# Weight splits of the token-major products written 32 bytes past a multiple of 64

## The chip, the cores and the metric

The kernel runs on one core of a Trainium2 chip. The metric is the device time of one execution in microseconds (us); lower is better. Three runs of the kernel before gave 1770.18 to 1772.55 us, with a median of 1770.89.

## The reference

One layer of a hybrid block on 256 tokens of width 2048, all in float32. A normalised input is multiplied by a wide matrix; the pieces go through four branches (a gated linear recurrence, attention with forgetting, a state-space scan, an RWKV recurrence); each branch's output is projected, gated and summed; then an output projection, a feed-forward part with a short convolution, and a gated embedding follow. Cut to the products:

```python
xn = rmsnorm(h, mix_norm[i])
proj = jnp.einsum('bsd,dn->bsn', xn, w_in[i])        # 14092 columns: gates, a, b, c, d
...
gates = jax.nn.sigmoid(g_raw).reshape(Bsz, S, N_BRANCH, D)
merged = gates[:, :, 0] * jnp.einsum('bsc,cd->bsd', branches[0], w_branch[i, 0])
for j in range(1, N_BRANCH):
    merged = merged + gates[:, :, j] * jnp.einsum('bsc,cd->bsd', branches[j], w_branch[i, j])
h = h + jnp.einsum('bsd,de->bse', merged, w_out[i])
...
u = causal_dwconv(jnp.einsum('bsd,df->bsf', hn, w_up[i]), ffn_conv_w[i], ffn_conv_b[i])
h = h + jnp.einsum('bsf,fd->bsd', jax.nn.gelu(u_gate) * u_val, w_down[i])
pg = jax.nn.sigmoid(jnp.einsum('bsd,de->bse', rmsnorm(h, ple_norm[i]), w_ple_gate[i]))
h = h + pg * jnp.einsum('bsq,qd->bsd', p[i], w_ple[i])
```

## The kernel before

Weights come from DRAM in chunks of 128 partitions by 1024 float32 (tile `wr`, four buffers, queue of SyncE). Every chunk is split in two float32r parts by `split` (line 213): ScalarE casts it to `wh` (line 217), VectorE writes the remainder to `wl` (line 218), each with three buffers. Activations are split in the same way, so that a product of float32 numbers becomes three float32r products: high by high, high by low and low by high.

There are two kinds of product, and both end in `mm`, whose matmuls carry line 132. Every matmul has a stationary operand of 128 by 128, loaded by an instruction of its own, and a moving one.

- `gemm_fm` (line 261), feature-major: the weights are stationary and the activations move. A tile `x`, `f`, `e` or `d` holds the high part of the 256 tokens and, behind it, the low part, so that `product` (line 244) needs one matmul of 512 columns with `wh` and one of 256 columns with `wl`. From the second k-tile on the order is `wl` (256), `wh` (512), so short and long matmuls alternate; two 512s meet where one output tile or one unit ends and the next begins.
- `gemm_tm` (line 309), token-major: the activations are stationary and the weights move. For each of the two token tiles and each of two k-tiles in a chunk there are three matmuls of 512 columns: `wh`, `wh`, `wl`. A chunk has 12. It serves the projection `w_v`, the gates `w_g` (16 units) and the branch projections `w_branch` (16 units), which together lie between about 160 and 835 us.

In the profile's rows the operand that moves is named first: `pg<-x,wh` moves `x` over a stationary `wh` (feature-major), `pg<-wh,x` moves `wh` over a stationary `x` (token-major). `sb` are buffers of the branches; `pg` and `pb` are banks of PSUM.

Priorities of a scheduler set the order of instructions on each engine: the weights' loads and splits (`lane("g")`) first, then the branches' work (`lane("b")`), then the products (`lane("m")`); the branches' matmuls are laid into the products' stream by `on_pe` (line 130).

Where operands lie: in the program as built, `wr`, `wh` and `wl` start at multiples of 64 bytes in their partition. An 8-column tile (`pad0`, line 162, 32 bytes) stands ahead of the pools of activations, so `x`, `f`, `e`, `d`, `s` and `sb` start 32 bytes past a multiple of 64; slices of them are whole multiples of 64 bytes apart. `cbr` and `R` start at multiples of 64.

Of the kernel before, what the change touches and what calls it, by code (L numbers as in the profile page):

```python
# [8 lines left out]
F32R = mybir.dt.float32r  # L9
# [5 lines left out]
P = 128  # L15
# [70 lines left out]
def body(tc, T, out, dbg=None):  # L86
# [51 lines left out]
    def mm(o, l, r, start=True, stop=True):  # L138
        on_pe(PE.matmul, o, l, r, start=start, stop=stop)
# [11 lines left out]
    def lane(name):  # L151
        prio[cur[0]] = tc.cur_priority
        cur[0] = name
        tc.cur_priority = prio[name]
# [3 lines left out]
    wp = ctx.enter_context(tc.tile_pool(name="wp", bufs=2))  # L158
# [20 lines left out]
    def gbank():  # L179
        return psG.tile([P, 512], F32, name="pg", tag="pg")  # L180
# [27 lines left out]
    def chunk(src, kn, cols, eng=None):  # L208
        wr = wp.tile([P, kn, cols], F32, name="wr", tag="wr", bufs=4)
        (eng or dma_w).dma_start(wr, src)  # L210
        return wr

    def split(wr, kn, cols):

        wh = wp.tile([P, kn, cols], F32R, name="wh", tag="wh", bufs=3)
        wl = wp.tile([P, kn, cols], F32R, name="wl", tag="wl", bufs=3)
        A.copy(wh, wr)  # L217
        V.tensor_tensor(wl, wr, wh.bitcast(F32), op=ALU.subtract)  # L218
        return [(wh[:, i], wl[:, i]) for i in range(kn)]
# [21 lines left out]
    def halves(x):  # L241
        return (x[:, :S], x[:, S:]) if not isinstance(x, tuple) else x
# [18 lines left out]
    def gemm_fm(W, xs, evac, each=None):  # L261
# [12 lines left out]
        while k0 < nk:  # L274
            kn = min(step, nk - k0)
            lane("g")
            if each is not None:
                kn = 1 if k0 < 4 else 2
            if each is None:
                w = chunk(W[k0 // step].rearrange("p (k n) -> p k n", k=kn), kn, ncol)  # L280
            else:
                w = chunk(W[k0:k0 + kn].rearrange("k p n -> p k n"), kn, ncol)
                each(k0, kn)
            w = split(w, kn, ncol)
            lane("m")
            for m in range(nm):
                ms = slice(m * P, m * P + P)
                for k in range(kn):
                    if not isinstance(xs[k0 + k], tuple):
                        product(pts[m], xs, k0 + k, nk, ms, w[k], not (each and m == 0))  # L290
                        continue
                    xh, xl = xs[k0 + k]
                    wh, wl = w[k]
                    first, last = k0 + k == 0, k0 + k == nk - 1
                    pt = pts[m][:, :S]
                    mm(pt, wh[:, ms], xh, start=first, stop=False)
                    mm(pt, wh[:, ms], xl, start=False, stop=False)
                    mm(pt, wl[:, ms], xh, start=False, stop=last)
                if hook[0]:
                    hook[0]()  # L300
            k0 += kn
# [7 lines left out]
    def gemm_tm(W, xs, evac):  # L309

        nk = len(xs)
        pts = [gbank() for _ in range(2)]
        for k0 in range(0, nk, 2):
            lane("g")
            w = split(chunk(W[k0 // 2].rearrange("p (k n) -> p k n", k=2), 2, 512), 2, 512)
            lane("m")
            for t in range(2):
                tsl = slice(t * P, t * P + P)
                for k in range(2):
                    xh, xl = halves(xs[k0 + k])  # L320
                    wh, wl = w[k]
                    first, last = k0 + k == 0, k0 + k == nk - 1
                    mm(pts[t], xh[:, tsl], wh, start=first, stop=False)
                    mm(pts[t], xl[:, tsl], wh, start=False, stop=False)
                    mm(pts[t], xh[:, tsl], wl, start=False, stop=last)
                if hook[0]:
                    hook[0]()
        lane("g")
        for t in range(2):
            evac(t, pts[t])  # L330
        lane("b")
# [688 lines left out]
    def small_logits():  # L1020
        lane("g")
        wt = []
        for i in range(2):
            wt += split(chunk(T["w_small"][i].rearrange("p (k n) -> p k n", k=8), 8, 64), 8, 64)
        lane("m")
        pt = gbank()
        for k in range(KD):
            xh, xl = halves(xs[k])
            wh, wl = wt[k]
            mm(pt[:64, :S], wh, xh, start=k == 0, stop=False)  # L1030
            mm(pt[:64, :S], wh, xl, start=False, stop=False)
            mm(pt[:64, :S], wl, xh, start=False, stop=k == KD - 1)
        lane("b")
        bcol = pc("logit_bias", 0)[:64]
        y = bslot()
        tt(y[:64], pt[:64, :S], R[:64], ALU.mult)
        ts(y[:64], y[:64], bcol, cc("sgn")[:64], ALU.add, ALU.mult)
        o = bc_.tile([64, S], F32, name="spo")
        w = [bslot()[:64] for _ in range(5)]
        softplus(y[:64], o, w)  # L1040
        spf = bc_.tile([4, S], F32, name="spf")
        A.copy(spf, o[32:36])
        raw["sp_dt"] = o[0:8]
        raw["sp_f"] = spf
# [50 lines left out]
    def evac_v(t, pt):  # L1095
        s = dslot()
        act(s, pt, AF.Identity, scale=rcol[:, t:t + 1])
        raw["v"].append(s)
    gemm_tm(T["w_v"], xs, evac_v)
    launch("b", fox)  # L1100
    proj("du", 12, 7)
# [11 lines left out]
    def gate_unit(j, u, early):  # L1113
        def ev_g(t, pt):
            if early:
                gates[u, t] = [bslot(), bslot()]
            else:
                s = wide()
                gates[u, t] = [s]
            n = 512 // len(gates[u, t])  # L1120
            for i, g in enumerate(gates[u, t]):
                act(g, pt[:, i * n:i * n + n], AF.Tanh, scale=rhalf[:, t:t + 1])
        gemm_tm(T["w_g"][4 * j + u], xs, ev_g)

    def branch_unit(j, u, first, last):
        def ev_z(t, pt):
            gs = gates.pop((u, t))
            n = 512 // len(gs)
            for i, g in enumerate(gs):
# [4 lines left out]
                else:  # L1134
                    add(merged[u, t][:, sl], merged[u, t][:, sl], g)
        gemm_tm(T["w_branch"][4 * j + u], ys[j], ev_z)
        if not last:
            return
# [132 lines left out]
    for u in range(8):  # L1271
        lane("g")
        w = split(chunk(T["w_ple"][u, 0].rearrange("p (k n) -> p k n", k=2), 2, S), 2, S)
# [83 lines left out]
```

## Time and profile before

| | before |
|---|---|
| median of three runs | 1770.89 us |
| profiled execution, its own time | 1767.91 us |
| its span, first to last instruction | 1766.0 us |
| TensorE busy | 1738.9 us, 98% |
| TensorE weight loads (beside the matmuls) | 1485.9 us, 84% |
| VectorE busy | 1219.1 us, 69% |
| ScalarE busy | 945.8 us, 54% |
| mean granted TensorE clock | 0.992 of full speed |

All durations in the text come from the one profiled execution. A matmul's row covers the time from its start to its modelled end, and the next one starts before that; the time from one start to the next is called its slot here.

### The profile page before, as it was taken

How to read it: one execution, taken by the hardware profiler on the slowest of the kernel's cores; microseconds unless marked ns; L12 is line 12 of the kernel's file. 1: busy time of each engine (PE TensorE's matmuls, PEld its weight loads, DVE VectorE, ACT ScalarE, POOL GpSimd, SP SyncE). 2: the span in 40 equal slices, each digit the busy share in tenths (PEclk: the TensorE clock that was granted, in tenths of full speed). 3: DMA queues.
4: the chain of work that ended last, by engine and by line, in shares of the span. 5: the costliest groups of instructions: out<-in, count | busy, mean ns of one | idle time of the engine just before them, and what ended most of it. 6: DMA issues, size and time to landing. Idle time of an engine off the chain costs nothing.

```text
span 1766.0 us, 25711 instructions
## 1 busy us (share of the span) xinstructions
PE 1738.9 (98%) x9733; PEld 1485.9 (84%) x9733; DVE 1219.1 (69%) x1895; ACT 945.8 (54%) x1398; POOL 102.7 (6%) x160
## 2 busy tenths in 40 slices
PE   8999999999999999989999999999999999999998
PEld 6888888888888778868888888888888888888887
DVE  7788667677789633356778777777777765555676
ACT  6576445556644333354556555555555544444454
POOL 4000000002320100000110000000000000000000
PEclk9999999999999989989999999999999999999999
DMA  7556556556675734445676555555556666555574
GB/s 273 170 169 197 166 170 218 190 188 201 206 220 178 249 126 143 142 151 179 217 231 196 191 189 190 188 188 191 190 190 191 212 209 196 193 191 188 175 225 135
DMA packets 98827, 336.01 MB, mean 190 GB/s; under 512 B 12330, under 2 KB 16592, under 8 KB 98704
## 3 DMA queue, kind: packets, MB, share of 16 engines
q1 hardware_dynamic: 90528, 310.94, 54.2%
q0 software_dynamic: 7456, 21.81, 4.2%
q8 instruction: 76, 1.25, 0.3%
q10 hardware_dynamic: 720, 1.63, 0.3%
q14 instruction: 47, 0.39, 0.1%
HBM read 324.85 MB, written 9.48 MB: 189 GB/s over the span
## 4 chain that ended last, share of the span: by engine, by line
PE 95%; DVE 2%; ACT 1%; DMA 1%; issue 1%; SPq 0%; POOL 0%; DVEq 0%; ACTq 0%
PE pg L132 90%; PE pb L135 4%; PE pb L132 1%; DVE wl L218 0%; DVE sb L100 0%; DMA d<-in_xT_dram 0%; ACT wh L217 0%; DMA d<-ssd_ac 0%; ACT sb L127 0%; DVE x L120 0%; DMA wr<-in_w_ax_dram 0%; ACT L127 0%; DVE s L100 0%; DVE e L116 0%; DVE sb L124 0%
## 5 line engine op out<-in xcount | busy, mean ns | idle before, releaser
L218 DVE TENSOR_TENSOR wl<-wr,wh 128x1024 fp32r<-128x1024 f32 (+1 forms) x592 | 717.2, 1213 | 455.7 <-ACT wh L217 441.4
L217 ACT CAST wh<-wr 128x1024 fp32r<-128x1024 f32 (+1 forms) x592 | 615.1, 1040 | 606.7 <-PE pg L132 511.2
L132 PE MATMUL pg<-x,wh 128*128 128x512 f32 (+1 forms) x2336 | 801.5, 390 | 2.4 <-DVE sb L100 2.4
L132 PE MATMUL pg<-x,wl 128*128 128x256 f32 (+1 forms) x2320 | 632.3, 283 | 9.1 <-DVE wl L218 9.1
L132 PEld LDWEIGHTS pg<-x,wh 128*128 128x128 f32 (+1 forms) x2336 | 432.5, 187 | 87.4 <-issue 2.4
L132 PEld LDWEIGHTS pg<-x,wl 128*128 128x128 f32 (+1 forms) x2320 | 437.1, 189 | 22.7 <-DVE wl L218 11.0
L132 PE MATMUL pg<-wh,x 128*128 128x512 f32 x1088 | 341.2, 403 | 4.9 <-ACT sb L127 4.9
L132 PEld LDWEIGHTS pg<-wh,x 128*128 128x128 f32 x1088 | 206.2, 191 | 53.7 <-ACT sb L127 5.2
L132 PE MATMUL pg<-f,wh 128*128 128x512 f32 x704 | 243.2, 390 | 0.0
L132 PE MATMUL pg<-wl,x 128*128 128x512 f32 x544 | 208.4, 405 | 1.1 <-DVE wl L218 1.1
L132 PE MATMUL pg<-f,wl 128*128 128x256 f32 x704 | 195.8, 282 | 0.0
L132 PEld LDWEIGHTS pg<-f,wh 128*128 128x128 f32 x704 | 131.7, 188 | 26.9
L132 PEld LDWEIGHTS pg<-f,wl 128*128 128x128 f32 x704 | 133.0, 189 | 1.0
L132 PEld LDWEIGHTS pg<-wl,x 128*128 128x128 f32 x544 | 103.8, 191 | 26.3 <-DVE wl L218 2.0
L258 ACT COPY s<-pg 128x256 f32<-128x256 f32 x136 | 50.6, 372 | 94.6 <-PE pg L132 94.6
L132 PE MATMUL pg<-wh,sb 128*128 128x512 f32 x256 | 78.6, 399 | 0.0
L120 DVE SCALAR_TENSOR_TENSOR s<-s,prm 128x254 f32<-128x254 f32 (+1 forms) x176 | 73.1, 478 | 0.0
L100 DVE TENSOR_TENSOR s<-s 128x256 f32<-128x256 f32 (+2 forms) x156 | 66.5, 448 | 1.8 <-ACT s L127 0.4
L100 DVE TENSOR_TENSOR s<-s,pg 128x256 f32<-128x256 f32 x136 | 56.7, 418 | 12.1 <-ACT s L258 8.5
L132 PEld LDWEIGHTS pg<-wh,sb 128*128 128x128 f32 x256 | 47.4, 188 | 11.4
L127 ACT ACT_TABLE_LOAD x39 | 50.0, 1283 | 1.9 <-PEq L1347 1.2
L127 ACT ACTIVATE s<-s,prm 128x256 f32<-128x256 f32 x88 | 48.1, 596 | 0.0
(236 smaller groups left out, 1300.6 us busy)
## 6 DMA issues: line engine op xcount, KB each, us to landing
wr<-in_w_up_dram SPq DMA_DIRECT2D x176, 512.0 KB, 3.4
wr<-in_w_g_dram SPq DMA_DIRECT2D x128, 512.0 KB, 3.6
wr<-in_w_down_dram SPq DMA_DIRECT2D x88, 512.0 KB, 4.3
wr<-in_w_p_dram SPq DMA_DIRECT2D x76, 512.0 KB, 3.6
wr<-in_w_branch_dram SPq DMA_DIRECT2D x32, 512.0 KB, 4.3
wr<-in_w_out_dram SPq DMA_DIRECT2D x32, 512.0 KB, 3.8
wr<-in_w_ple_gate_dram SPq DMA_DIRECT2D x32, 512.0 KB, 4.5
wr<-in_w_v_dram SPq DMA_DIRECT2D x8, 512.0 KB, 4.2
```

Source lines behind the costliest of these rows:

```text
L100: V.tensor_tensor(o, a, b, op=op)
L120: V.scalar_tensor_tensor(o, a, s, b, op0=op0, op1=op1)
L127: A.activation(o, i, f, **kw)
L132: return f(*a, **kw)
L135: f(*a, **kw)
L217: A.copy(wh, wr)
L218: V.tensor_tensor(wl, wr, wh.bitcast(F32), op=ALU.subtract)
L258: A.copy(o, pt[:, S:])
```

## The change

`split` takes an offset. The two parts are now allocated as 1040 columns (4160 bytes) instead of 1024, and the split is written into the columns from `off` on. `gemm_tm` passes 8 columns, 32 bytes; all other callers keep 0.

```diff
-    def split(wr, kn, cols):
-
-        wh = wp.tile([P, kn, cols], F32R, name="wh", tag="wh", bufs=3)
-        wl = wp.tile([P, kn, cols], F32R, name="wl", tag="wl", bufs=3)
+    def split(wr, kn, cols, off=0):
+
+        part = lambda n: wp.tile([P, 1040], F32R, name=n, tag=n, bufs=3)[
+            :, off:off + kn * cols].rearrange("p (k n) -> p k n", k=kn)
+        wh, wl = part("wh"), part("wl")
         A.copy(wh, wr)
         V.tensor_tensor(wl, wr, wh.bitcast(F32), op=ALU.subtract)
         return [(wh[:, i], wl[:, i]) for i in range(kn)]
...
-            w = split(chunk(W[k0 // 2].rearrange("p (k n) -> p k n", k=2), 2, 512), 2, 512)
+            w = split(chunk(W[k0 // 2].rearrange("p (k n) -> p k n", k=2), 2, 512), 2, 512, 8)
```

The order of the instructions on every engine, the buffers they use and their waits are the same before and after; only addresses differ (and line numbers from 217 on, by one). `wh` and `wl` of a token-major product start 32 bytes past a multiple of 64, those of a feature-major one at a multiple of 64 as before. Each of the six buffers is 64 bytes longer, so that what is allocated behind them lies 384 bytes further on, six times 64.

## Rows read from the trace of the kernel before

**Rows 1.** The page's first part: busy time of each engine, with its share of the span and its instructions.

```profile
span 1766.0 us, 25711 instructions
PE 1738.9 (98%) x9733; PEld 1485.9 (84%) x9733; DVE 1219.1 (69%) x1895; ACT 945.8 (54%) x1398; POOL 102.7 (6%) x160
```

**Rows 2.** The chain that ended last: shares by engine (from the page), and its two longest pieces of matmuls (from the chain in order of time: start, duration, what, how many).

```profile
PE 95%; DVE 2%; ACT 1%; DMA 1%; issue 1%; SPq 0%; POOL 0%; DVEq 0%; ACTq 0%
...
493.91 87.02 PE pg L132 x373
...
935.89 729.78 PE pg L132 x4203
```

**Rows 3.** Groups of TensorE by line, operands and shape (busy us, mean ns of one, idle before): first in the stretch 494 to 581 us, where all products are token-major, then in 936 to 1660 us, where all are feature-major.

```profile
L132 PE MATMUL pg<-wh,x 128*128 128x512 f32 x202 | 59.7, 395 | 0.0
L132 PE MATMUL pg<-wl,x 128*128 128x512 f32 x101 | 36.3, 396 | 0.0
...
L132 PE MATMUL pg<-x,wh 128*128 128x512 f32 x1383 | 474.0, 391 | 0.0
L132 PE MATMUL pg<-x,wl 128*128 128x256 f32 x1381 | 374.7, 281 | 0.0
L132 PE MATMUL pg<-f,wh 128*128 128x512 f32 x704 | 243.2, 390 | 0.0
```

**Rows 4.** The same groups over the whole span: the four token-major ones, then the feature-major one of `d`, and the branches' plain float32 matmuls of 256 columns (each of these stands as two records).

```profile
L132 PE MATMUL pg<-wh,x 128*128 128x512 f32 x1088 | 341.2, 403 | 4.9 <-ACT sb L127 4.9
L132 PE MATMUL pg<-wl,x 128*128 128x512 f32 x544 | 208.4, 405 | 1.1 <-DVE wl L218 1.1
L132 PE MATMUL pg<-wh,sb 128*128 128x512 f32 x256 | 78.6, 399 | 0.0
L132 PE MATMUL pg<-wl,sb 128*128 128x512 f32 x128 | 47.6, 397 | 0.0
...
L132 PE MATMUL pg<-d,wh 128*128 128x512 f32 x128 | 45.0, 395 | 0.0
L135 PE MATMUL pb<-sb,e 128*128 128x256 f32 x32 | 8.8, 378 | 0.0
```

**Rows 5.** Feature-major 512s that follow each other. The timeline of TensorE at the border of two units (start, duration, what; rows of one kind that follow each other are one row), then the group of the second and third of the three 512s there, then the timeline at the first use of `d`.

```profile
948.60 0.86 PE L132 MATMUL pg<-x,wh 128*128 128x512 f32 x3
949.30 0.40 PE L132 MATMUL pg<-x,wl 128*128 128x256 f32 x2
...
L132 PE MATMUL pg<-x,wh 128*128 128x512 f32 x2 | 0.6, 396 | 0.0
...
835.52 0.64 PE L132 MATMUL pg<-d,wh 128*128 128x512 f32 x2
836.00 0.40 PE L132 MATMUL pg<-d,wl 128*128 128x256 f32 x2
```

**Rows 6.** The timeline of a token-major stream: four matmuls and the start of the next, and the loads of the same four.

```profile
541.57 1.09 PE L132 MATMUL pg<-wh,sb 128*128 128x512 f32 x4
542.50 0.39 PE L132 MATMUL pg<-wl,sb 128*128 128x512 f32 x1
...
541.33 0.89 PEld L132 LDWEIGHTS pg<-wh,sb 128*128 128x128 f32 x4
```

**Rows 7.** The timeline where a branch's matmul (`sb` moving) stands between token-major ones, the mean of that branch matmul (one of its kind in its window), and the timeline where a feature-major stream passes into a token-major one.

```profile
744.49 0.28 PE L135 MATMUL pb<-sb,exc 128*128 128x256 f32 x1
744.61 0.39 PE L132 MATMUL pg<-wl,x 128*128 128x512 f32 x1
...
L135 PE MATMUL pb<-sb,exc 128*128 128x256 f32 x1 | 0.3, 277 | 0.0
...
183.01 0.39 PE L132 MATMUL pg<-x,wh 128*128 128x512 f32 x1
183.24 1.09 PE L132 MATMUL pg<-wh,x 128*128 128x512 f32 x4
```

**Rows 8.** Groups of ScalarE and VectorE by shape over the whole span. `wh`, `wl`, `wr`, `cbr` and `R` are at offset 0, `f`, `s` and `exc` at 32.

```profile
L217 ACT CAST wh<-wr 128x1024 fp32r<-128x1024 f32 x578 | 606.4, 1050 | 590.3 <-PE pg L132 497.2 <-issue 57.3 <-ACT s L127 22.9
L217 ACT CAST wh<-wr 128x512 fp32r<-128x512 f32 x14 | 8.7, 618 | 16.4 <-PE pg L132 14.0 <-DMA wr<-in_w_ax_dram 2.0 <-PE pb L132 0.4
L223 ACT CAST f<-s 128x256 fp32r<-128x256 f32 x44 | 15.5, 401 | 0.0
L451 ACT CAST exc<-cbr 128x128 fp32r<-128x128 f32 x2 | 0.5, 294 | 0.0
...
L218 DVE TENSOR_TENSOR wl<-wr,wh 128x1024 fp32r<-128x1024 f32 x578 | 706.9, 1224 | 440.7 <-ACT wh L217 426.5 <-PE pg L132 8.2 <-PE pb L135 0.5
L100 DVE TENSOR_TENSOR f<-s,f 128x256 fp32r<-128x256 f32 x44 | 16.6, 419 | 0.0
L100 DVE TENSOR_TENSOR s<-s 128x512 f32<-128x512 f32 x16 | 10.6, 685 | 0.1
L100 DVE TENSOR_TENSOR s<-s,R 128x256 f32<-128x256 f32 x104 | 44.0, 425 | 3.2
```

**Rows 9.** The stretch 318 to 800 us, most of the token-major stage: busy time of PE, PEld, DVE, ACT and POOL (with instructions), granted clock, share of DMA, GB/s; and who waited for whom in it (us in total, times, longest).

```profile
318.00:800.00 482.00, 473.51 (x2558) 381.53 (x2557) 294.78 (x414) 230.51 (x322) 51.95 (x78) 0.98 0.57 180
...
ACT wh L217 <- PE pg L132: 167.6, 98, 3.3
PE pg L132 <- DVE wl L218: 1.1, 1, 1.1
```

## The prediction

> **What bounds the kernel now.** I read the busy times first [rows 1]: TensorE works 1738.9 of 1766.0 us, VectorE 69%, ScalarE 54%. The chain of waits says the same from the end backwards [rows 2]: TensorE owns 95% of it, and its two longest pieces are 87.02 us with 373 matmuls and 729.78 us with 4203, each without a break. So the time is the number of matmuls times the slot of one, and a change that touches no instruction can act only through the slot, or by making an engine beside TensorE so slow that TensorE waits for it.
>
> The slot has to be read with care, because a matmul's row covers its whole pipeline and neighbours overlap. In the long piece 729.78 / 4203 = 173.6 ns, so a pair (512 and 256 columns) takes 347.3 ns, while the two means of that stretch are about 391 and 281 [rows 3], together 672. Each row therefore overlaps the next by about (672 - 347.3) / 2 = 162 ns, and slot = mean - 162. For the token-major products the other piece gives it directly: 87.02 / 373 = 233.3 ns, and their means of 395 and 396 less 162 agree [rows 2, 3].
>
> **The change part by part.** No instruction, wait or transfer is added, removed or moved; three things differ.
>
> First, the moving operand of the token-major products (`gemm_tm`) starts at 32 bytes past a multiple of 64 where it started at 0. These are 1088 + 544 + 256 + 128 = 2016 matmuls of 512 columns [rows 4]; at 233.3 ns they are 470 us of the span. Every nanosecond on their slot is 2.0 us, and 0.2% of the time (3.5 us, about what a measurement of this kernel can tell from no change) is 1.75 ns. The feature-major products already read a moving operand 32 bytes off (`x`, `f`, `e`, `d`), and their 512-column matmul looks cheaper: mean 390 or 391 against 395, a slot of about 228.5 [rows 3]. Taken as the effect of the offset, this would give 2016 x (233.3 - 228.5) = 9.7 us back. But their neighbours differ: there a 512 follows a 256. The place to look is where a feature-major stream happens to run three 512s in a row, at the border of two units [rows 5]. The first starts at 948.60 and the next short one at 949.30, so three slots take 0.70 us, 233 each; the second and third have a mean of 396, slot 234, with the moving operand 32 bytes off. A token-major stream, at 0, takes 0.93 us for four, 232.5 each [rows 6]. The slot goes with the matmul before it and not with the offset. I take 0 for this part. The ends are -9.7 us (rows 3 read at face value) and, upwards, the slowest undisturbed 512-column slots in the trace, two in 0.48 us or 240 ns at the first use of `d` [rows 5]: 2016 x 6.7 = +13.5 us.
>
> Second, in these products both operands now have the same offset: the moving weights and the activations that are loaded as stationary operand while it streams (a load starts one slot ahead of its matmul [rows 6]) stand 32 bytes off. Before, one of the two was always at 0 and the other at 32, in both kinds of product, so the pairing is new for a stream of 512-column matmuls. Near it are two places. At 744.49 a 256-column matmul of the branches (moving `sb` at 32) stands between token-major ones, and while it streams, an `x` at 32 is loaded [rows 7]: the next starts 0.12 us later, and its row has 277 ns, where the usual pairing has 281 [rows 3]. At 183.01 a feature-major 512 at 32 is followed by a token-major one, whose `x` at 32 is loaded meanwhile: 0.23 us to the next start [rows 7]. That is 230 after a 256, against 228.5 for the old pairing, or 1.5 x 2016 = 3 us if it were a rule; the 256-column case points the other way (277 against 281). I take 0.
>
> Third, ScalarE writes `wh` and VectorE writes `wl` 32 bytes off, and VectorE reads one input at 0 and one at 32. ScalarE's cast takes 618 ns for 512 elements and 1050 for 1024 at offset 0, so 0.84 ns each and 402 for 256; with both sides at 32 it takes 401, and from 0 to 32 with 128 elements 294, where the line gives 294 [rows 8]. No cost. VectorE's subtraction takes 1224 for 1024 at 0; at 32 it takes 419 for 256 and 685 for 512, so 1217 by that line, and with inputs at 32 and 0 (`s<-s,R`) 425 against 419 [rows 8], at most 6 ns in 256, 24 in 1024. That lies beside TensorE: a pair of k-tiles keeps it busy for 12 x 233 = 2.8 us, the split takes ScalarE 1.05 and VectorE 1.22, ScalarE waits 167.6 us in the stage for TensorE to hand a buffer back, and TensorE waits 1.1 us for `wl` [rows 9]. Without that cover, 168 splits at 24 ns would be 4 us.
>
> Buffers are 64 bytes longer and what comes after them moves by 384 bytes. Tiles at very different places have nearly one mean for the same matmul, `x` 391, `f` 390 and `d` 395 with its slow first use [rows 3 to 5], so 0.
>
> The sum is 0: 1767.9 us for an execution like the profiled one (span 1766.0 and 1.9 around it), and 1770.9 for the median of the runs, which stands 3.0 us above the profiled one.
>
> Here the Trainium skill speaks for a larger effect than I forecast: "TensorE: Matmul & The Clock Gate", section "Back-to-back issue gap", puts a 512-column matmul at about 216 ns at the full clock, where this trace has 233 [rows 2]. If the present offset were what holds the slot up, the Trainium skill's figure would make the sum 2016 x 17.3 = -35 us, an estimate; rows 5, with 512s at the other offset no quicker, speak against it.
>
> **Rivals.** (a) The offset pays. Mechanism: the moving read at 0 costs some ns, and at 32 the slot falls to that of the feature-major 512, 228.5: -9.7 us, 1761. In its extreme form more goes: the plain fp32 matmuls of 256 columns with both operands at 32 have a mean of 378, slot 216 [rows 4], and if 512 float32r columns came down to that it would be -35 us, 1736. (The figure of the Trainium skill above comes out at the same place.) For it: the means of rows 3, and that those fp32 matmuls have both operands at 32. Against it: rows 5, 512s at 32 with a slot of 233 to 234, and the fp32 form has half as many columns.
>
> (b) Equal offsets collide. Mechanism: the moving read and the weight load beside it, one at 0 and one at 32 in every product before, now fall on the same phase of 64 bytes and get in each other's way, in 2016 matmuls. Priced at the slowest slot the trace shows, 240 [rows 5], it is +13.5 us, 1784; it decides from 1.75 ns a matmul on. For it: all products of the kernel before avoid this pairing, so its price was hardly seen. Against it: rows 7, two matmuls with this pairing at the usual slot.
>
> (c) The split becomes the bound: the write 32 bytes off would have to bring VectorE from 294.8 busy us in the 482 of rows 9 close to TensorE's 473.5: 1.2 us more for each split of 1.22, doubled. Rows 8 show nothing of it; it has 1 of the 11 below.
>
> **How the numbers follow.** Forecast (0) 74%; (a) 15%, of which 3 for the extreme form; (b) and (c) 11%. The predicted time is the forecast's, 1770.9. The forecast's own range is its 0.2%, 1767.4 to 1774.4. To hold 8 in 10, the range goes down to the likelier form of (a), 1761, and a little up into (b), where a small collision of 2 ns would end at 1775. Faster by over 0.2% 0.15, within 0.74, slower 0.11.
>
> **What would show it.** In the profile after, the four token-major groups keep means of 395 to 398 in an undisturbed stretch such as 494 to 581 us, and the chain's piece there keeps 233 ns a matmul. (a) shows as means near 390 and a token-major stage (318 to 800) shorter by some 7 us; (b) as means above 397 in those groups alone, with the feature-major ones at 390 and 282 as now; (c) as TensorE waiting for `wl`, with the mean of the 1024-element forms above 1224. I am wrong if the token-major slot moves by 2 ns or more either way, or if feature-major stretches change pace, for which no step above allows.

## The result and the profile after

After: 1774.01 us, median of 20 runs (1770.37 to 1775.87); before, timed beside them: 1769.88 us, also of 20 (1766.46 to 1773.47). The ratio is 1.0021, with a 95% interval of 1.0014 to 1.0028: slower by 3.7 us (2.5 to 5.0) by the ratio, by 4.1 us between the two medians. That is inside the forecast range and at the edge of "no change" (0.2%), which the interval does not exclude. The profiled execution took 1772.25 us, against 1767.91 before; the granted clock was 0.991 of full speed, against 0.992.

The page of the kernel after: its busy times, the chain's shares by engine, and the two groups of the split.

```profile
span 1770.3 us, 25711 instructions
PE 1744.1 (99%) x9733; PEld 1482.9 (84%) x9733; DVE 1219.1 (69%) x1895; ACT 945.1 (53%) x1398; POOL 102.7 (6%) x160
...
PE 92%; DVE 4%; issue 2%; ACT 1%; DMA 1%; SPq 0%; POOL 0%; DVEq 0%; ACTq 0%
...
L219 DVE TENSOR_TENSOR wl<-wr,wh 128x1024 fp32r<-128x1024 f32 (+1 forms) x592 | 716.6, 1212 | 458.7 <-ACT wh L218 444.0
L218 ACT CAST wh<-wr 128x1024 fp32r<-128x1024 f32 (+1 forms) x592 | 614.6, 1039 | 610.9 <-PE pg L132 512.0
```

Against [rows 1], TensorE is busy 5.2 us longer with the same 9733 matmuls, in a span that is 4.3 us longer. VectorE and ScalarE stand where they stood. So what changed is the pace of the matmuls. The chain in order of time, as in [rows 2], shows in which direction.

```profile
497.58 30.54 PE pg L132 x132
...
934.90 734.41 PE pg L132 x4203
```

The feature-major piece has the same 4203 matmuls and takes 734.41 us where it took 729.78: 4.6 us more, in products that the diff does not touch. The token-major piece, once 373 matmuls long, is broken off after 132, at 30.54 / 132 = 231.4 ns each where they took 233.3. The groups by line, tile and shape say the same, in 494 to 581 us (as in [rows 3]) and in 936 to 1640 us (there up to 1660; over 936 to 1640 the rows of `x,wh` and `f,wh` before have 391 and 390 ns, as in [rows 3], and `f,wl` 282).

```profile
L132 PE MATMUL pg<-wh,x 128*128 128x512 f32 x198 | 58.8, 394 | 0.0
L132 PE MATMUL pg<-wl,x 128*128 128x512 f32 x100 | 35.7, 395 | 0.0
...
L132 PE MATMUL pg<-x,wh 128*128 128x512 f32 x1379 | 475.9, 394 | 0.0
L132 PE MATMUL pg<-f,wh 128*128 128x512 f32 x637 | 221.2, 393 | 0.0
L132 PE MATMUL pg<-f,wl 128*128 128x256 f32 x637 | 175.9, 280 | 0.0
```

Token-major rows are 1 ns shorter than before, feature-major 512s 3 ns longer. These means round away what matters, so the slots below are taken from the start times themselves: the mean from one matmul's start to the next one's, over the whole trace, where the next is a matmul with a weight part too, leaving out gaps of 300 ns and more. There are 2016 token-major matmuls, 3068 feature-major 512s after a 256, and 3076 256s after a 512.

| slot, ns | before | after |
|---|---|---|
| token-major, 512 after 512 | 233.15 | 231.21 |
| feature-major, 512 after 256 | 228.98 | 231.87 |
| feature-major, 256 after 512 | 118.59 | 118.61 |

1.94 x 2016 = 3.9 us are gained and 2.89 x 3068 = 8.9 us lost: +5.0 by slots, where 3.7 were timed. Setting the start of the same matmul in the two traces side by side shows it along the program (times of before, and how much later after is):

```
us before   183.5  318.0  494.2  620.0  800.1  936.1  1300.1  1665.2  1760.0
after, us    +3.9   +4.8   +3.7   +1.1   -1.4   -1.0    +1.5    +3.6    +4.3
```

Stretches with mostly feature-major products (up to 318 us and from 835 us on) lose steadily; the token-major stage between them wins back all that was lost, and 1.4 us more by 800 us, before the feature-major rest spends it.

### The profile page after: what moved, and what is told of

The parts are those of the page before. It is cut to its first block, busy times and chain, and to the rows that moved or that the text cites. A ratio compares the mean times of both kernels' runs of the same rounds, so it can differ in the third digit from the quotient of the medians.

```text
span 1770.3 us, 25711 instructions
## 1 busy us (share of the span) xinstructions
PE 1744.1 (99%) x9733; PEld 1482.9 (84%) x9733; DVE 1219.1 (69%) x1895; ACT 945.1 (53%) x1398; POOL 102.7 (6%) x160
## 4 chain that ended last, share of the span: by engine, by line
PE 92%; DVE 4%; issue 2%; ACT 1%; DMA 1%; SPq 0%; POOL 0%; DVEq 0%; ACTq 0%
PE pg L132 87%; PE pb L135 4%; DVE wl L219 1%; PE pb L132 1%; DVE e L100 1%; DVE e L900 0%; ACT L127 0%; DVE sb L100 0%; ACT wh L218 0%; ACT sb L127 0%; DMA d<-in_xT_dram 0%; DMA d<-ssd_ac 0%; DVE x L120 0%; DMA wr<-in_w_ax_dram 0%; DVE s L100 0%
## 5 line engine op out<-in xcount | busy, mean ns | idle before, releaser
L132 PE MATMUL pg<-x,wh 128*128 128x512 f32 (+1 forms) x2336 | 810.0, 394 | 2.3 <-DVE sb L100 2.3
L132 PE MATMUL pg<-wh,x 128*128 128x512 f32 x1088 | 337.3, 399 | 4.9 <-ACT sb L127 4.9
```

What stands on the lines that cost most here:

```text
L132: return f(*a, **kw)
```

## The experiments

What had to be told apart: whether the slots moved because of the offset itself, because everything behind the buffers moved by 384 bytes, because the buffers became 65 x 64 bytes long, or because of how far apart the two operands of TensorE stand. In each edit, lines are against the kernel before unless the change, or another run, is named. "Distance" is where the moving operand stands less where the stationary one stands, modulo 256 bytes, worked out from the addresses of the built programs.

**Longer buffers without the offset.** The change, with the offset taken out again:

```diff
-            w = split(chunk(...), 2, 512, 8)
+            w = split(chunk(...), 2, 512)
```

> The buffers keep their length of 1040 columns, but the split is written at 0 everywhere. In the profile after, the token-major slot fell by 2 ns (means 399/402 against 403/405) and the feature-major 512s rose by 3 (mean 394 and 393 against 392 and 390). All feature-major addresses here are those of the change, so the theory that buffer length (or the shift of what lies behind) slows them expects means of 393 to 394 again. Token-major: if the 32 bytes brought the 2 ns, they are lost and the run ends 4 us above the change (ratio to before 1.004 to 1.005); if the phases of the longer buffers brought them, it ends with the change (1.002).

Measured: 1777.69 us, 1.0039 (1.0027 to 1.0052). Its chain:

```profile
496.92 87.05 PE pg L132 x373
...
938.02 734.40 PE pg L132 x4203
```

The token-major piece is that of before (87.02), the feature-major one that of after (734.41). So without the offset feature-major is as slow as in the change (232.02 ns a slot): the length does it, or the shift that comes with it, and what the change wins in token-major comes from the offset.

**The shift alone.** Buffers as before, 384 bytes of padding behind them:

```diff
-    pad.tile([P, 8], F32, name="pad0")
+    pad.tile([P, 104], F32, name="pad0")
```

> Buffers and offsets as before, and 384 bytes of padding ahead of the activations, which so lie where the change put them. Theory S, the shift of the activations slows the feature-major 512s: mean 393 to 394, ratio 1.004 to 1.006. Theory P, the length of the weight buffers does it (their starts are spread over 0, 64 and 128 bytes of 256): mean 390 to 392, ratio 0.999 to 1.001. Token-major slot as before in both (means 403/405), unless it depends on the distance of the two operands too.

Measured: 1769.94 us, 0.9999 (0.9990 to 1.0009); slots 229.70 (512 after 256) and 233.53 (token-major), a little up, while the 256 after a 512 falls from 118.6 to 118.0. The shift is not the cause of the time, so the length is.

**The change with the shift undone modulo 512.** 128 bytes more, so that activations stand again where they stood within 512 bytes:

```diff
-    pad.tile([P, 8], F32, name="pad0")
+    pad.tile([P, 40], F32, name="pad0")
```

> The change with 128 bytes more padding, so that activations are 512 bytes past their place before: the same place within 512 bytes. Theory P: feature-major means stay at 393 to 394, ratio 1.001 to 1.003. Theory S: they return to 390 to 392 while the token-major gain stays, ratio 0.997 to 0.998.

Measured: 1779.61 us, 1.0046 (1.0034 to 1.0058), above what either theory expected; the feature-major slot is 234.07, worse than in the change, the token-major one 231.02 as there. Putting the activations back does not help while the weights' buffers stand at places unlike one another.

**The offset without the length.** The weights' parts get a pool of their own behind the 32 bytes of padding; buffers keep 1024 columns, and all splits, the feature-major ones too, stand 32 bytes off like the activations:

```diff
     pad.tile([P, 8], F32, name="pad0")
+    wq = ctx.enter_context(tc.tile_pool(name="wq", bufs=3))
...
-        wh = wp.tile([P, kn, cols], F32R, name="wh", tag="wh", bufs=3)
-        wl = wp.tile([P, kn, cols], F32R, name="wl", tag="wl", bufs=3)
+        wh = wq.tile([P, kn, cols], F32R, name="wh", tag="wh", bufs=3)
+        wl = wq.tile([P, kn, cols], F32R, name="wl", tag="wl", bufs=3)
```

> The 8-column tile of padding moved ahead of wh and wl: buffers of 1024 columns, activations exactly where they were before, every wh and wl 32 bytes off, in feature-major products too. Theory O, two operands at one offset within 64 bytes are read a little quicker (token-major 233.2 to 231.2): token-major means 401/403, and feature-major 512s not slower (390 to 392); ratio 0.996 to 0.998. Rival, equal offsets collide: feature-major and token-major means rise by 3 or more, ratio above 1.005. If neither moves, the change's 2 ns came from the buffers' length: ratio 1.000.

Measured: 1774.79 us, 1.0028 (1.0017 to 1.0038). Its chain, and groups of the two stretches:

```profile
491.72 68.38 PE pg L132 x301
...
932.14 739.21 PE pg L132 x4203
```

```profile
L132 PE MATMUL pg<-wh,x 128*128 128x512 f32 x200 | 57.7, 389 | 0.0
...
L132 PE MATMUL pg<-x,wh 128*128 128x512 f32 x1371 | 478.0, 399 | 0.0
```

The ratio lies between the two that were expected, because the two kinds of product move in opposite directions. A token-major matmul takes 68.38 / 301 = 227.2 ns where it took 233.3, and its row 389 ns for 395; the feature-major piece takes 9.4 us more and its row 399 ns for 391. Equal places go with a faster 512 after a 512 and a slower 512 after a 256.

**No padding at all**, so that activations and weights' parts both start at 0:

```diff
-    pad.tile([P, 8], F32, name="pad0")
```

> The 8-column padding left out: activations at 0 of 64 bytes, as the weights, both kinds of product, nothing else. Theory D, the distance alone counts: the same as with everything at 32 (token-major 228, feature-major 512 after 256 at 235, ratio 1.002 to 1.004). Rival, a place of 32 itself is what is quick or slow: token-major stays at 233 since its moving operand has not moved, and feature-major changes by its own: ratio off that range, above 1.006 if the pairing at 0 is slow in both.

Measured: 1774.26 us, 1.0022 (1.0013 to 1.0031); slots 235.05, 117.35 and 228.13, as with both at 32 (234.89, 117.15, 227.99); the chain's feature-major piece is the same to 0.01 us:

```profile
933.31 739.22 PE pg L132 x4203
```

So 32 bytes off is neither good nor bad; only the distance between the two counts.

**The change with buffers of 9 x 512 bytes.** All six buffers now stand at one place within 512, so only token-major products get a new distance. The room comes from one buffer of scratch:

```diff
-        part = lambda n: wp.tile([P, 1040], ...
+        part = lambda n: wp.tile([P, 1152], ...
-    sp = ctx.enter_context(tc.tile_pool(name="sp", bufs=12))
+    sp = ctx.enter_context(tc.tile_pool(name="sp", bufs=11))
```

> Token-major splits 32 bytes off as in the change, but buffers of 1152 columns (4608 bytes, nine times 512), so that every buffer keeps the place within 512 bytes that it had before; activations too. Room for it comes from one buffer less of the 512-column scratch tiles (11 for 12). Theory D (what counts is the distance of the moving operand from the weights loaded beside it: equal places help a run of 512s and hurt a 512 after a 256): token-major slot 228 as in the run with the offset alone, feature-major 512 after 256 at 229 as before: 2016 x 5.2 = 10 us less than the same kernel without the offset, ratio to before 0.993 to 0.996. Rival: the gain of 5 ns in that run came from the feature-major products being shifted too, or needs unpadded buffers: token-major 231 to 233, ratio 0.998 to 1.001.

Measured: 1762.81 us, 0.9959 (0.9946 to 0.9973). And the kernel before with 11 scratch buffers, as the control:

> The control for the run before it: the kernel before with 11 scratch buffers for 12, nothing else. All matmuls at their places within 512 bytes, same order on TensorE. If the buffer isn't missed, ratio 0.999 to 1.001 and means as before (390 and 282; 403 to 405); if it is, TensorE waits for it and the ratio rises by what the waits show.

Measured: 1768.96 us, 0.9996 (0.9987 to 1.0004); every slot is within 0.1 ns of before. The gain is the distance's. The chain of the kernel with 1152 columns:

```profile
491.18 38.18 PE pg L132 x168
...
930.35 729.80 PE pg L132 x4203
```

The feature-major piece is that of before to 0.02 us, the token-major slot 38.18 / 168 = 227.3 ns. By slots, (233.15 - 228.21) x 2016 = 10 us were to come; 7.3 came by the ratio. The rest is mostly given back in the token-major products: the gaps of 300 ns and more after one, which the slots leave out, are 126 with 49.7 us in all, in the control 112 with 42.0 us. A part of that is TensorE's wait for `wl`, 2.8 us in 318 to 800 us where the control has 1.2; all of it falls in 494 to 581 us.

```profile
L132 PE MATMUL pg<-wl,x 128*128 128x512 f32 x98 | 34.9, 395 | 2.8 <-DVE wl L219 2.8
```

**Which step of length is enough?** The same with 1056 columns (33 x 128 bytes) and 1088 columns (17 x 256):

```diff
-        part = lambda n: wp.tile([P, 1152], ...
+        part = lambda n: wp.tile([P, 1056], ...      (the other: 1088)
```

> As the run that won (token-major splits 32 bytes off, 11 scratch tiles), with buffers of 1056 columns, 4224 bytes, 33 times 128: each buffer starts 128 bytes further within 512 than the one before it. If places within 128 bytes are all that counts, token-major keeps 228 and feature-major 229 after a 256, ratio to before 0.995 to 0.997. If the step has to be 256 or 512, the slots stand between those and the change's (231 each), ratio 0.998 to 1.003.

> The same with buffers of 1088 columns, 4352 bytes, 17 times 256: every second buffer starts 256 bytes further within 512. If places within 256 bytes are all that counts: token-major 228, feature-major 229, ratio 0.995 to 0.997. If it takes 512: token-major and feature-major both a little above, ratio 0.997 to 1.001.

Measured: 1770.90 us, 1.0006 (0.9997 to 1.0015) for 1056, slots 230.47 (512 after 256) and 231.33 (token-major); 1760.89 us, 0.9952 (0.9939 to 0.9966) for 1088, slots 228.99 and 228.18. Places 256 bytes apart are as good as equal ones, 128 are not. The 1088-column kernel has the lowest ratio of the study, 8.5 us under before, though its interval overlaps that of the 1152-column one. Its chain:

```profile
490.05 49.34 PE pg L132 x217
...
928.16 729.78 PE pg L132 x4203
```

Here, too, 8.5 of the 10 us came. The chain by line in 470 to 620 us, first of the control, then of the 1088-column kernel:

```profile
by line: PE pg L132 92.9%; PE pb L135 5.8%; DVE wl L218 0.8%; DVE s L100 0.5%; issue 0.1%; DVEq L218 0.0%
```

```profile
by line: PE pg L132 69.1%; issue 7.9%; PE pb L135 6.0%; DVE wl L219 5.9%; DVE e L100 4.7%; DVE e L900 3.9%; DVE s L100 1.3%; DVE s L120 1.3%; DVEq L219 0.0%
```

Where the chain ran through TensorE alone, a quarter of it now runs through VectorE, the split among it, and issue. The likely reading is that the faster matmuls catch up with the recurrences beside them. The waits that the profile shows are short: for `wl`, 2.4 us in 318 to 800 us, and the gaps of 300 ns and more are 126 with 48.6 us. In the change itself, too, only 56.5% of the chain in 470 to 620 us are the products' matmuls.

**Distance, or place within 64 bytes?** With 1088 columns the token-major split moved to 96 and to 160 bytes: the place within 64 bytes stays equal to that of the activations, the distance within 256 becomes 64 and 128.

```diff
-            w = split(chunk(...), 2, 512, 8)
+            w = split(chunk(...), 2, 512, 24)      (the other: 40)
```

> The kernel with buffers of 1088 columns (17 x 256 bytes), but the token-major split 96 bytes into its buffer where it was 32: moving and stationary operand then have the same place within 64 bytes, as in the change, and stand 64 apart within 256. If the distance within 256 bytes is what counts (equal place wanted), the token-major slot leaves 228.2 ns and comes to 231 to 235, and the time rises by 6 to 14 us to 1767 to 1775. If the place within 64 bytes is what counts, and the change lost half of its gain only because its six buffers stand at places unlike one another, the slot stays at 228 and the time at 1761. Feature-major 512s after a 256 stay at 229 by both.

> The same with the token-major split 160 bytes into its buffer: equal place within 64 and 32 bytes, 128 apart within 256. Distance within 256: slot 231 to 235, time 1767 to 1775; if half of 256 counts as equal, 228 and 1761. Place within 64 bytes: 228 and 1761.

Measured: 1765.12 us, 0.9976 (0.9963 to 0.9988), slot 229.93; and 1769.47 us, 0.9996 (0.9987 to 1.0006), slot 232.80. The place within 64 bytes falls as an explanation; the distance within 256 stands, but my price for 64 was wrong: I expected 231 to 235, and it costs 1.4 ns over equal places in products with `x`, not 3 or more. At 128 the slot is nearly that of before, and so is the chain's piece:

```profile
495.91 86.97 PE pg L132 x373
```

**Another distance for feature-major.** With 1088 columns, the feature-major splits 96 bytes into their buffers (token-major as in the change):

```diff
-    def split(wr, kn, cols, off=0):
+    def split(wr, kn, cols, off=24):
```

> The kernel with buffers of 1088 columns, token-major split at 32 bytes as there, and the feature-major split 96 bytes into its buffer where it was at 0: stationary weights and moving activations have the same place within 64 bytes and stand 64 apart within 256. If the place within 64 bytes is what counts, it is the pairing of equal places: a 512 after a 256 takes 235 ns and the 256 117.3, so 3068 x (6.0 - 1.3) = +14 us, 1775. If the distance within 256 bytes counts, it is a distance not tried alone: between 227 and 235 ns, and 229 would say that only distance 0 is bad there. Token-major 228 by both.

Measured: 1780.26 us, 1.0061 (1.0044 to 1.0078): the 512 after a 256 takes 234.34 ns and the 256 119.15, while token-major keeps 227.97.

```profile
937.74 741.99 PE pg L132 x4203
```

For this pairing it is nearly as bad a place as the equal one (234.9 and 235.05), and the 256s don't get cheaper as they do at distance 0, so the time is above the 1775 that was expected for equal places. It has the highest ratio of the study, though its interval overlaps that of the run with the shift undone.

## What the slots follow

Sorted by distance, all kernels whose six buffers stand at one place within 256 bytes agree. These are means over each group of matmuls in the trace of the run named by its distance (a dash where no run has it; `sb` stands 64 bytes from `x` within 256, so most runs give two distances).

| distance, bytes | 0 | 32 | 64 | 96 | 128 | 160 | 192 | 224 |
|---|---|---|---|---|---|---|---|---|
| token-major 512 after 512, `x` stationary, ns | 227.7 to 228.0 (five runs) | - | 229.3 | 233.4 | 232.7 | - | - | 233.1 |
| the same, `sb` stationary | - | 233.3 | 229.2 to 229.4 (five runs) | - | 232.7 | 234.2 | 233.2 | - |
| feature-major 512 after 256, `x` moving | 235.6, 235.8 | 229.0 | - | - | - | 229.6 | 234.4 | - |
| the 256 after it, `x` moving | 117.4, 117.7 | 118.8 to 119.0 | - | - | - | 118.2 | 119.4 | - |

Where the token-major rows meet (64, 128), different buffers of different runs give the same slot to 0.1 ns. In feature-major products the operand's kind matters as well: `f` takes 228.5 at 32, near `x`, but 232.9 at 0. `d` was seen at distances that `x` lacks: 233.6 at 96, 230.9 at 128 and 230.7 to 231.0 at 224. Before, `x` stood at 224 in token-major and at 32 in feature-major: nearly the worst for the one, the best of those tried for the other. But the difference between the 233 and the 229 of the kernel before is not one of distance: at 32 a 512 takes 233.3 after a 512 and 229.0 after a 256.

In the change the buffers are 65 x 64 bytes long, so the six stand at four different places: token-major distances are 0, 64, 128 and 192, feature-major ones 32, 96, 160 and 224. Its averages, 231.2 and 231.9, lie inside what the table spans. But the table is not a rule for each single matmul there: its token-major matmuls at distance 0 take 230.9 with `x`, not 227.9. Where neighbours come from buffers at unlike places, the places of the neighbours enter, and the feature-major 512s of the change show it. Among those of `x` whose own weights stand at distance 32, as before, 457 stand between two 256s whose weights are at 160, and 163 between two whose weights are at 96, all within one chunk. The first take 229.5 ns, the second 235.2; the same matmuls took 228.8 and 229.2 in the kernel before. So the place of a matmul's own weights does not settle its slot, and the places of the weights used just before and after it count. By what rule, and whether it is the next one's that count, which are loaded while the matmul streams, is open; in an even stream all are at one distance.

## Why the prediction was right and wrong

The range held the time, but by luck: the reasons behind the zero were wrong in two places, and the two errors were of opposite sign, 8.9 us lost and 3.9 us won by slots. The top of the range was there for a small collision in the token-major products, and those became faster.

**What held.** That a change which touches no instruction can act only through the slot or through the split. That the split has cost and cover to spare: the 1024-element forms take 1049 ns on ScalarE and 1223 on VectorE, against 1050 and 1224 [rows 8], although 168 of the 578 are now written 32 bytes off; in 494 to 581 us, where all of them are, VectorE takes 1216 ns for 1217.

```profile
L219 DVE TENSOR_TENSOR wl<-wr,wh 128x1024 fp32r<-128x1024 f32 x578 | 706.4, 1223 | 443.5 <-ACT wh L218 430.0 <-PE pg L132 8.1
...
L218 ACT CAST wh<-wr 128x1024 fp32r<-128x1024 f32 x578 | 605.9, 1049 | 594.2 <-PE pg L132 497.8 <-issue 58.8 <-ACT s L127 23.4
```

And ScalarE's wait for TensorE in 318 to 800 us, which I named as the cover, is 163.0 us for 167.6 [rows 9].

```profile
ACT wh L218 <- PE pg L132: 163.0, 96, 3.3
...
PE pg L132 <- DVE wl L219: 1.3, 2, 1.1
```

**The step that failed first: "Buffers are 64 bytes longer and what comes after them moves by 384 bytes", "so 0".** I argued it from equal means of `x`, `f` and `d` in the kernel before. But all of those means came with the weights' buffers at one place within 256 bytes, and I looked at where the tiles lie, not at how far a tile is from the weight loaded against it. `d`, which I excused with "its slow first use", was the hint: it stands at distance 224, and its slots in the kernel before are 230.7 against 229.0 for `x`. The length alone costs 6.9 us (1.0039), the shift nothing.

**The second: "The slot goes with the matmul before it and not with the offset. I take 0 for this part."** Its first half holds for the old places: 233 after a 512, 229 after a 256. The second half does not follow. In [rows 5] the feature-major 512s stand at distance 32 and in [rows 6] the token-major ones (with `sb`) at 32 as well; I compared them as opposite offsets, but they stand at the same distance, so that they could not show what a new distance does.

**The third: the pairing, "I take 0".** It was the right question, asked of the wrong rows. At the border of [rows 7] the `x` loaded meanwhile stands at distance 0, but the `wh` that the matmul itself uses at 32, as ever. A stream in which both are at 0 takes 235.6 after a 256 and 227.9 after a 512: a border of one matmul showed neither, and the sign turns with the neighbour. Such a border hardly prices a stream at all: in the last run, where the `wh` stand at 192 and a stream takes 234.4, its three such borders take 230 to 231.

**The rivals.** (a), priced at -9.7 us, had the right size for the wrong reason: 228.2 instead of the forecast 228.5 is what the token-major slot reaches, though by distance and not by the offset, and only with buffers a multiple of 256 bytes long. In the change it reached 231.2. Its extreme form, 216 ns, did not come: the fastest stream takes 227.7. The Trainium skill ("TensorE: Matmul & The Clock Gate", section "Back-to-back issue gap") gives the 216 ns that the prediction names for a matmul by itself, and about 131 ns for a stream of loads and matmuls; the streams here are at neither. (b), equal places that collide, has its place and sign wrong: for a 512 after a 512 it is a gain of 5 ns, for a 512 after a 256 a loss of 6. (c) did not happen: TensorE waits 1.3 us for `wl` in 318 to 800 us, for 1.1 before.

**My own test** said that I am wrong "if feature-major stretches change pace, for which no step above allows". They did, by 2.9 ns a slot. The token-major slot moved by 1.9 ns, where I had set 2 as the mark.

## What to carry to other kernels

Where TensorE is the bound and each matmul has a weight load of its own, the two operands' addresses can be a knob, here of 2 to 3% of the slot: lay all buffers of one operand at one place modulo 256 bytes, and then try the distance to the other operand, separately for each pattern of long and short matmuls. A change of a buffer's length by anything that is no multiple of 256 bytes re-deals these places for every user of the pool, also for code that the diff does not touch. To price such a thing, compare rows by the distance of the two operands, not by the place of one, and only in streams whose neighbours stand alike.

## What the runs showed of the hardware

The slot of a matmul depends on where its two operands stand to each other. The Trainium skill ("TensorE: Matmul & The Clock Gate", section "Step-by-step: what each phase is for") says that two separate read ports feed the moving operand and the weight load, so that loading does not take bandwidth from the running matmul. Here the same instructions, in the same order, with the same loads, took 227.9 or 233.1 ns in token-major streams and 229.0 or 235.6 after a 256, by nothing but the two operands' distance in memory. That the load and the moving read are what meet there is the likeliest reading, but it was only argued, and the page's statement on bandwidth was not tested by itself; that the slot follows the two operands' places is measured.

It was also not expected that the interaction has opposite signs for the two patterns, and a period: places 256 bytes apart act as equal (1088 columns, 0.9952), 128 apart do not (1056 columns, 1.0006). What in the memory or the array makes 256 the period, why the neighbour's length turns the sign, steps finer than 32 bytes, and the rule by which a mixed set of places sets the slot of a single matmul were not settled by these runs.
